# Latent attention of a two-layer decoder: the order of its query and key products, the split of the query weights, a shorter rotation and head loads in two parts

## The chip, the cores and the metric

The kernel runs on one core of a Trainium2 chip. The metric is device time in microseconds (us), the median of several runs. The profile shows one execution: PE is TensorE (matrix products), PEld its weight loads, DVE is VectorE, ACT is ScalarE, POOL is GpSimd, and SP is the engine that only issues transfers. ACT and POOL can issue transfers too. Each engine works through its own instructions in order; an instruction that waits holds up all that stand behind it on its engine.

## The reference

Two layers over 1024 positions of width 1024. The first layer mixes tokens by latent attention with 12 heads, the second by a sliding window; both have four heads of attention over a memory beside it and a squared-ReLU MLP behind. The change touches the first layer's mixer:

```python
def mla_mixer(hn, positions, w_in, q_norm_g, kv_norm_g, w_uq, w_ukv):
    proj = hn @ w_in
    c_q, c_kv, k_r, q_cross = ...
    q = (rmsnorm(c_q, q_norm_g) @ w_uq).reshape(b, s, 12, 96)
    q = concatenate([q[..., :64], rope(q[..., 64:], positions)])
    kv = (rmsnorm(c_kv, kv_norm_g) @ w_ukv).reshape(b, s, 12, 128)
    k_nope, v = kv[..., :64], kv[..., 64:]
    k = concatenate([k_nope, rope(k_r)])
    return causal_dense_attention(q, k, v), q_cross
```

`rope` rotates 32 values as two halves of 16: `x1 * cos - x2 * sin` and `x1 * sin + x2 * cos`. The softmax is over `q @ k.T / sqrt(96)` under a causal mask.

## The kernel before

Everything is float32. For products that need its precision, each operand is split into a high part (rounded to the format that PE takes at full rate) and a low part, the rest, and three products are summed: high by high, high by low, low by high. `split` (L96) makes the two parts: an ACT copy, scaled if there is a scale, writes the high part, and a DVE operation writes the low part. `part` (L931) does the same for a result in PSUM and sends the low part to DRAM through SP's queue, from a ring of four buffers named `lo`.

The stages of the first layer, with their times in the profile:

- `a_in` (34 to 131 us) projects each tile of 128 positions, normalises, rotates the 32 shared key values with `rope` (L317) and transposes. `rope` takes four DVE products of half width and two POOL additions.
- The values and the attention over the memory (131 to 176 us).
- The queries and keys (176 to 246 us), L945 to L1007, which is what the change rewrites. There are three kinds of product. The plain keys come from the compressed keys, pair of heads by pair of heads (`pskn`, j = 0 to 5, 12 products of 512 columns each, in one of two large PSUM buffers). The rotated part of the queries comes for each tile of positions t = 0 to 7 (`q_rope`, `psqr`, 9 products of 384 columns); `rope` rotates it on DVE and POOL, and two tiles later `q_ropeT` (`psqt`) transposes it on PE and parts it. The plain queries come for each pair of heads and half of the positions (`q_nope`, `psqn`, 12 times 9 products of 512 columns). The program writes them down as: all keys, then all rotated queries, then the plain queries. The order in which they stand on PE is made from this by a planner that fills a place where it expects an instruction not to be ready.
- The query weights are loaded by `load_cols` (L702) in 18 pieces, 9 of the rotated columns (`wqr`) and 9 of the plain ones (`wqn`), each through one of two buffers (`wr` in the profile, tag `wraw`). With `pool_too`, POOL scales the piece in place (L712), ACT rounds it (L713), POOL subtracts (L714), and only then is the buffer free for the next load, which SP issues (L707). `wqr` takes the place of the value weights; `wqn` takes the place of the key weights `wkn` as a whole, and one new tile.
- The attention proper (246 to 438 us) goes through 12 heads of 12 blocks each. A head's operands are four tiles (high and low of query and key, 96 rows and one row for a correction) in one of three sets of buffers. `head_tiles(h)` (L875) has SP issue up to eight loads into them: high and low, plain and rotated rows; the third set lies in space that the weights leave free only when the last query product is done. Before a head is attended to, its row maxima are found: `row_max(h, i)` (L900) multiplies high by high for the i-th tile of queries, and a DVE operation (L912) takes the maximum; when all eight are there, `max_row(h)` (L888) transposes them on PE (`psxt`), ACT copies them, and a transfer from ACT's queue puts them into the correction row. In the attention the order of PE's products is written out by hand: block n = 12h + j issues its scores (`pss`), then the row maxima that the table `WHEN` (L1195) puts there for a later head, then, every sixth block, a batch of products with the values (`pso`). Where a block crosses the diagonal, DVE adds the mask (L1076) for heads 2 to 8, PE for the others. POOL sums the probabilities (L1091).
- The sums of each head go through `den`; `rc_split` (L1168) inverts them for a group of heads on DVE, and `rc_mul` (L1176) multiplies the outputs, also on DVE, at places given by block number (L1234 to L1238).
- From 438 us on: the output projection, the MLP and the whole second layer, which the change leaves alone.

Of the kernel before, what the change touches and what calls it, by code (L numbers as in the profile page):

```python
# [19 lines left out]
P = 128  # L20
# [35 lines left out]
def trunk(  # L56
# [260 lines left out]
    def rope(pl, src, dst, t, nh, ab=None):  # L317

        rope_ct[0] += 1
        c = cosb[:, t : t + 1, :].to_broadcast([P, nh, 16])  # L320
        s = sinb[:, t : t + 1, :].to_broadcast([P, nh, 16])
        if ab is None:
            ab = [pl.tile([P, nh, 16], F32, tag=f"r{e}", bufs=2, name=f"r{e}{rope_ct[0]}") for e in "ab"]
        a, b = ab
        x1, x2 = src[:, :, 0:16], src[:, :, 16:32]
        V = nc.vector
        V.tensor_tensor(dst[:, :, 0:16], x1, c, ALU.mult)
        V.tensor_tensor(a, x2, s, ALU.mult)
        V.tensor_tensor(dst[:, :, 16:32], x1, s, ALU.mult)
        V.tensor_tensor(b, x2, c, ALU.mult)  # L330
        nc.gpsimd.tensor_tensor(dst[:, :, 0:16], dst[:, :, 0:16], a, ALU.subtract)
        nc.gpsimd.tensor_tensor(dst[:, :, 16:32], dst[:, :, 16:32], b, ALU.add)
# [369 lines left out]
    def load_cols(src, nk, w, outs, g, pool_too=False):  # L702

        for kt in range(nk):
            for i in range(3):
                raw = wu.tile([P, 4, w], F32, tag="wraw", bufs=2, name=f"wr{w}_{outs[0][1]}_{kt}_{i}")
                nc.sync.dma_start(out=raw.rearrange("p h c -> p (h c)"), in_=src[kt * P : (kt + 1) * P, i * 4 * w : (i + 1) * 4 * w])  # L707
                for dst, c0, n in outs:
                    o = [d[:, i * 4 * n : (i + 1) * 4 * n].rearrange("p (h c) -> p h c", c=n) for d in dst[kt]]
                    r = raw[:, :, c0 : c0 + n]  # L710
                    if pool_too:
                        nc.gpsimd.tensor_scalar(r, r, g[:, kt : kt + 1], None, ALU.mult)  # L712
                        nc.scalar.activation(o[0], r, AF.Copy)  # L713
                        nc.gpsimd.tensor_tensor(o[1], r, f32(o[0]), ALU.subtract)  # L714
                    else:
                        split(r, *o, scale=g[:, kt : kt + 1])
                yield
# [5 lines left out]
    loading = load_cols(mla_w_ukv[0], 2, 128, [(wkv, 64, 64), (wkn, 0, 64)], g_kv)  # L723

    CQC, CKR = 640, 896
    def a_in(t):
# [10 lines left out]
             [f1[:, t % 2, MLA_IN + 16 * i : MLA_IN + 16 * i + 16].rearrange("p (h c) -> p h c", h=1) for i in range(2)])  # L737
# [180 lines left out]
    kn = [kq[j // 4][:, j % 4, :] for j in range(6)]  # L918
    qr = [kq[1][:, 2, :], kq[1][:, 3, :], raw_tile([P, S], "qr2")]
# [58 lines left out]
    def q_ropeT(t):  # L978
# [197 lines left out]
    def rc_mul(c):  # L1176
# [30 lines left out]
    for n in range(len(seq) + 2):  # L1207
# [1146 lines left out]
```

## Time and profile before

| | |
|---|---|
| median of three runs | 2097.43 us (2095.31 to 2098.25) |
| profiled execution, own time | 2094.01 us |
| its span | 2092.2 us, so 1.8 us lie around it |
| mean granted clock | 0.997 |
| PE busy | 98% of the span |
| DVE, ACT, POOL busy | 68%, 51%, 13% |

The tables of stretches list, for a piece of the span, each engine's busy time and the number of its instructions, then the clock that PE was granted (1.00 is full speed), the busy share of the 16 DMA engines and the rate moved. The tables of waits list who waited for whom: total us, how many times, and the longest. In a timeline a row is start, duration, engine, line, operation, output and inputs with their shapes, the count, and in brackets the idle time before it with what ended it.

### The profile page before, as it was taken

How to read it: one execution, taken by the hardware profiler on the slowest of the kernel's cores; microseconds unless marked ns; L12 is line 12 of the kernel's file. 1: busy time of each engine (PE TensorE's matmuls, PEld its weight loads, DVE VectorE, ACT ScalarE, POOL GpSimd, SP SyncE). 2: the span in 40 equal slices, each digit the busy share in tenths (PEclk: the TensorE clock that was granted, in tenths of full speed). 3: DMA queues.
4: the chain of work that ended last, by engine and by line, in shares of the span. 5: the costliest groups of instructions: out<-in, count | busy, mean ns of one | idle time of the engine just before them, and what ended most of it. 6: DMA issues, size and time to landing. Idle time of an engine off the chain costs nothing.

```text
span 2092.2 us, 29674 instructions
## 1 busy us (share of the span) xinstructions
PE 2057.0 (98%) x10035; PEld 1677.8 (80%) x10035; DVE 1415.6 (68%) x2841; ACT 1072.0 (51%) x2349; POOL 276.9 (13%) x397
## 2 busy tenths in 40 slices
PE   8999899999999999999999999999999999999998
PEld 6987676678888888888888888778888888888887
DVE  8765555565977777976558534666977776976665
ACT  7554244465755544444445435766755444444453
POOL 1004355630000000000001133420000000000000
PEclk9999999999999999999999999999999999999999
DMA  6304645442344546944433534542345446944342
GB/s 224 104 7 125 197 101 138 122 162 81 136 149 158 166 146 230 331 136 154 141 116 106 151 98 126 140 132 86 124 155 165 162 141 231 330 144 156 117 123 88
DMA packets 192780, 308.61 MB, mean 148 GB/s; under 512 B 18863, under 2 KB 77684, under 8 KB 192628
## 3 DMA queue, kind: packets, MB, share of 16 engines
q1 hardware_dynamic: 184368, 287.97, 43.8%
q0 software_dynamic: 4144, 13.14, 1.7%
q10 hardware_dynamic: 4116, 5.61, 1.0%
q8 instruction: 79, 1.29, 0.3%
q14 instruction: 73, 0.60, 0.1%
HBM read 196.25 MB, written 89.57 MB: 137 GB/s over the span
## 4 chain that ended last, share of the span: by engine, by line
PE 92%; DVE 2%; ACT 2%; DMA 1%; POOL 1%; issue 1%; SPq 0%; ACTq 0%; DVEq 0%; POOLq 0%
PE psy L1926 6%; PE psy L1927 6%; PE psy L1928 6%; PE psu L1590 5%; PE psu L1589 5%; PE psu L1588 5%; PE psz L1926 4%; PE psz L1927 4%; PE psz L1928 4%; PE psv L1590 4%; PE psv L1589 4%; PE psv L1588 4%; PE pss L1044 3%; PE pswo L109 3%; PE pswo L111 3%; PE pswo L110 3%
## 5 line engine op out<-in xcount | busy, mean ns | idle before, releaser
L99 ACT ACTIVATE g<-i 128x512 fp32r<-128x512 f32 x79 | 49.9, 631 | 103.7 <-PE psy L1927 52.2
L1926 PE MATMUL psy<-g 128*128 128x512 f32 x256 | 100.0, 390 | 0.0
L1927 PE MATMUL psy<-g 128*128 128x512 f32 x256 | 99.7, 389 | 0.0
L1928 PE MATMUL psy<-g 128*128 128x512 f32 x256 | 99.7, 389 | 0.0
L1078 ACT ACTIVATE p<-pss 128x512 f32<-128x512 f32 (+2 forms) x144 | 64.2, 491 | 68.2 <-PE pss L1044 31.9
L912 DVE CUSTOM_DVE_ANT_0 psx<-psx,wide 128x1024 f32<-128x1024 f32 (+7 forms) x96 | 72.9, 765 | 37.6 <-PE psx L910 36.7
L1091 POOL TENSOR_TENSOR acc<-p,acc 128x512 f32<-128x512 f32 (+2 forms) x96 | 89.4, 938 | 33.4 <-ACT p L1078 29.5
L100 DVE TENSOR_TENSOR g<-i,g 128x512 fp32r<-128x512 f32 x79 | 55.5, 703 | 49.5 <-ACT g L99 49.5
L99 ACT ACTIVATE uh<-i 128x512 fp32r<-128x512 f32 x66 | 41.7, 632 | 88.1 <-PE psz L1927 39.4
L99 ACT ACTIVATE i<-mr 128x512 fp32r<-128x512 f32 x78 | 47.8, 628 | 71.9 <-PE psy L1927 23.0
L100 DVE TENSOR_TENSOR uh<-i,uh 128x512 fp32r<-128x512 f32 x66 | 45.5, 690 | 48.8 <-ACT uh L99 48.8
L1926 PE MATMUL psz<-g 128*128 128x512 f32 x192 | 74.7, 389 | 0.0
L1927 PE MATMUL psz<-g 128*128 128x512 f32 x192 | 74.7, 389 | 0.0
L1928 PE MATMUL psz<-g 128*128 128x512 f32 x192 | 74.7, 389 | 0.0
L1487 ACT ACTIVATE mr<-mr,gcol 128x256 f32<-128x256 f32 (+1 forms) x160 | 63.8, 476 | 12.7 <-DMA mr<-in_mlp_w_up_dram 12.7
L2046 POOL TENSOR_TENSOR wsr<-wsr,gcol 128x1024 f32<-128x1024 f32 x12 | 23.4, 1947 | 342.5 <-ACT i L99 274.9
L100 DVE TENSOR_TENSOR i<-mr,i 128x512 fp32r<-128x512 f32 x78 | 53.5, 686 | 20.9 <-ACT i L99 20.8
L1808 DVE TENSOR_TENSOR mqq<-mqf,mqq 128x512 f32<-128x512 f32 x64 | 43.1, 686 | 22.4 <-DMA mqf<-in_mlp_w_down_dram 22.3
L1044 PE MATMUL pso<-p,v 128*64 128x256 f32 (+1 forms) x480 | 56.4, 380 | 0.0
L1928 PEld LDWEIGHTS psy<-g 128*128 128x128 f32 x256 | 48.0, 188 | 10.0
L1926 PEld LDWEIGHTS psy<-g 128*128 128x128 f32 x256 | 48.1, 188 | 9.9
L1927 PEld LDWEIGHTS psy<-g 128*128 128x128 f32 x256 | 48.1, 188 | 9.8
(661 smaller groups left out, 6775.3 us busy)
## 6 DMA issues: line engine op xcount, KB each, us to landing
i<-hd SPq DMA_DIRECT2D x154, 256.0 KB
hd<-uh SPq DMA_DIRECT2D x76, 256.0 KB
hd<-ul SPq DMA_DIRECT2D x76, 256.0 KB
mr<-in_mlp_w_up_dram SPq DMA_DIRECT2D x36, 512.0 KB
hd<-x SPq DMA_DIRECT2D x72, 256.0 KB
mr<-hd SPq DMA_DIRECT2D x70, 256.0 KB
d<-in_mlp_w_up_dram SPq DMA_DIRECT2D x32, 512.0 KB
mqf<-in_mlp_w_down_dram SPq DMA_DIRECT2D x32, 512.0 KB
```

Of the source, the lines that this page charges most:

```text
L99: a = nc.scalar.activation(hi, src, AF.Copy)
L100: d = nc.vector.tensor_tensor(lo, src, f32(hi), ALU.subtract)
L912: nc.vector.tensor_tensor_reduce(ps[:, :n], ps[:, :n], wide[h > 1][:, S - n :], -1.0, 3.0e38, ALU.add, ALU.min, accum_out=m)
L1044: last_mm[0:1] = [nc.tensor.matmul(*args, skip_group_check=True, **kw).ins]
L1078: masked[0:1] = [nc.scalar.activation(p[:, c0:], ps, AF.Exp, scale=SC).ins]
L1091: nc.gpsimd.tensor_tensor(a[:, c0:], p[:, c0:], (a if q is None else q)[:, c0:], ALU.add)
L1588: nc.tensor.matmul(ps, wh[:, k, :], xh[:, k, :], start=p in (1, 2, 5) and k == 0, stop=False, skip_group_check=True)
L1589: nc.tensor.matmul(ps, wh[:, k, :], xl[:, k, :], start=False, stop=False, skip_group_check=True)
L1590: nc.tensor.matmul(ps, wl[:, k, :], xh[:, k, :], start=False, stop=k == 3, skip_group_check=True)
L1926: nc.tensor.matmul(ps, ah[:, j, :], bh, start=start, stop=False, skip_group_check=True)
L1927: nc.tensor.matmul(ps, ah[:, j, :], bl, start=False, stop=False, skip_group_check=True)
L1928: nc.tensor.matmul(ps, al[:, j, :], bh, start=False, stop=k == NP - 1, skip_group_check=True)
```

## The change

The rotation works on both halves at once: two DVE products of full width (by cosine and by sine) instead of four of half width; POOL's two additions stay.

The query weights are split as all others are: ACT scales and rounds, DVE scales and subtracts. POOL computes nothing there any more and issues the loads instead of SP. All nine rotated pieces are written down before the first key product. The plain pieces 0 and 1 of each group take the place of the key weights column by column, as soon as the products that read those columns are done, and come in the order in which the queries need them.

The products alternate in the program: keys 0 to 2, then for each tile a rotated product with, after t = 0, 1, 2, keys 3 to 5, and after t = 4, 5, 6 a plain query. The rotated queries' three transposed blocks lie side by side and are parted in one go (384 columns) rather than two (256 and 128).

A head's loads come in two parts, first the high tiles, one step later the low ones, with the constant rows for the correction behind the low ones. The first row maxima of head 0 come three plain queries later. In `WHEN`, row maxima 3 to 0 come one block earlier, the transpose of the maxima one block later, and head 2's first two row maxima one block later. The normalisation of the first two groups of heads starts 4 and 3 blocks later, of the third one block later.

```diff
-        c = cosb[:, t : t + 1, :].to_broadcast([P, nh, 16])
-        s = sinb[:, t : t + 1, :].to_broadcast([P, nh, 16])
+        c = cosb[:, t : t + 1, :].to_broadcast([P, 2 * nh, 16])
+        s = sinb[:, t : t + 1, :].to_broadcast([P, 2 * nh, 16])
...
-        V.tensor_tensor(dst[:, :, 0:16], x1, c, ALU.mult)
-        V.tensor_tensor(a, x2, s, ALU.mult)
-        V.tensor_tensor(dst[:, :, 16:32], x1, s, ALU.mult)
-        V.tensor_tensor(b, x2, c, ALU.mult)
-        nc.gpsimd.tensor_tensor(dst[:, :, 0:16], dst[:, :, 0:16], a, ALU.subtract)
-        nc.gpsimd.tensor_tensor(dst[:, :, 16:32], dst[:, :, 16:32], b, ALU.add)
+        nc.vector.tensor_tensor(flat(dst), flat(src), c, ALU.mult)
+        nc.vector.tensor_tensor(flat(ab), flat(src), s, ALU.mult)
+        nc.gpsimd.tensor_tensor(dst[:, :, 0:16], dst[:, :, 0:16], ab[:, :, 16:32], ALU.subtract)
+        nc.gpsimd.tensor_tensor(dst[:, :, 16:32], dst[:, :, 16:32], ab[:, :, 0:16], ALU.add)
...
-    def load_cols(src, nk, w, outs, g, pool_too=False):
...
+    def load_cols(src, todo, w, outs, g, dma):
+
+        for kt, i in todo:
+            raw = wu.tile([P, 4, w], F32, tag="wraw", bufs=2, name=f"wr{w}_{outs[0][1]}_{kt}_{i}")
+            dma.dma_start(out=raw.rearrange("p h c -> p (h c)"), in_=src[kt * P : (kt + 1) * P, i * 4 * w : (i + 1) * 4 * w])
+            for dst, c0, n in outs:
+                o = [d[:, i * 4 * n : (i + 1) * 4 * n].rearrange("p (h c) -> p h c", c=n) for d in dst[kt]]
+                split(raw[:, :, c0 : c0 + n], *o, scale=g[:, kt : kt + 1])
+            yield
...
-    def head_tiles(h):
+    def head_tiles(h, lo):
...
-        if h in (1, 2):
-            head_ones(h)
-        for t, n, rope in ((kh, kn[h // 2][r, :], krh_d), (qh, qn[h // 2][r, :], qr[h // 4][e, :]), (kl, kn_d[r_, :], krl_d), (ql, qn_d[r_, :], qr_d[e_, :])):
+        for t, n, rope in ((kl, kn_d[r_, :], krl_d), (ql, qn_d[r_, :], qr_d[e_, :])) if lo else ((kh, kn[h // 2][r, :], krh_d), (qh, qn[h // 2][r, :], qr[h // 4][e, :])):
             nc.sync.dma_start(out=f32(t[0:64]), in_=n)
...
+        if h in (1, 2) and lo:
+            head_ones(h)
...
-    kn = [kq[j // 4][:, j % 4, :] for j in range(6)]
-    qr = [kq[1][:, 2, :], kq[1][:, 3, :], raw_tile([P, S], "qr2")]
+    kn = [kq[j // 4][:, j % 4, :] for j in range(5)] + [raw_tile([P, S], "kn5")]
+    qr = [kq[1][:, 1 + j, :] for j in range(3)]
...
-    for j in range(6):
-        if j == 1:
-            wqr = rows(wpair(wu, 3, 384, "wqr", "b"), 3)
-            for _ in load_cols(mla_w_uq[0], 3, 96, [(wqr, 64, 32)], g_q, True):
-                pass
+    wqr = rows(wpair(wu, 3, 384, "wqr", "b"), 3)
+    for _ in load_cols(mla_w_uq[0], [(kt, i) for kt in range(3) for i in range(3)], 96, [(wqr, 64, 32)], g_q, nc.gpsimd):
+        pass
+    wqn = wkn + rows(wpair(wu2, 1, 768, "wqn2", "c"), 1)
+    loading = load_cols(mla_w_uq[0], [(kt, i) for i in range(3) for kt in range(3)], 96, [(wqn, 0, 64)], g_q, nc.gpsimd)
+
+    def k_nope(j):
...
-        part(kq[1][:, 2:4, sl], pt[:, 0 : 2 * P].rearrange("p (k c) -> p k c", k=2), qr_d[0 : 2 * P, sl].rearrange("(k p) c -> p k c", p=P))
-        part(qr[2][:, sl], pt[:, 2 * P : 3 * P], qr_d[2 * P : 3 * P, sl])
-
+        part(kq[1][:, 1:4, sl], pt.rearrange("p (k c) -> p k c", k=3), qr_d[:, sl].rearrange("(k p) c -> p k c", p=P))
+
+    for j in range(3):
+        k_nope(j)
     for t in range(NT):
         q_rope(t)
-        for _ in range(1 + (t < 2)):
-            next(loading, None)
+        if t < 3:
+            k_nope(t + 3)
+        if t < 5:
+            for _ in range(2 if t < 4 else 1):
+                next(loading, None)
         if t > 1:
             q_ropeT(t - 2)
-    q_nope(0, 0)
+        if t in (4, 5, 6):
+            q_nope((t - 4) // 2, t % 2)
     q_ropeT(NT - 2)
-    q_nope(0, 1)
+    q_nope(1, 1)
     q_ropeT(NT - 1)
-    head_tiles(0)
-    for n in range(2, 12):
+    for n in range(4, 12):
         q_nope(n // 2, n % 2)
-        for i in range(2 * n - 4, min(2 * n - 2, NT)):
-            row_max(0, i)
         if n == 4:
-            head_tiles(1)
-        if n == 8:
+            head_tiles(0, 0)
+        if n == 5:
+            head_tiles(0, 1)
+        if n == 7:
+            head_tiles(1, 0)
+        if n == 9:
+            head_tiles(1, 1)
+        if 4 < n < 9:
+            for i in range(2 * n - 10, 2 * n - 8):
+                row_max(0, i)
+        if n == 9:
             max_row(0)
...
-        1: ((4, 0), (3, 1), (2, 2), (1, 3), (0, 4), (8, 6)),
-        2: ((7, -5), (6, -4), (5, -1), (4, 1), (3, 2), (2, 3), (1, 4), (0, 5), (8, 6)),
+        1: ((4, 0), (3, 1), (2, 2), (1, 3), (0, 4), (8, 7)),
+        2: ((7, -4), (6, -3), (5, -1), (4, 1), (3, 1), (2, 2), (1, 3), (0, 4), (8, 7)),
+        3: ((7, -5), (6, -4), (5, -1), (4, 1), (3, 1), (2, 2), (1, 3), (0, 4), (8, 7)),
...
-            if j == 0 and h + 2 < H:
-                head_tiles(h + 2)
+            if j < 2 and h + 2 < H:
+                head_tiles(h + 2, j)
...
-        for c in range(3):
-            if n == GRP[c + 1] * NB + (8 if c == 2 else 10):
+        for c, (a, b) in enumerate(((6 * NB + 14, 6 * NB + 17), (11 * NB + 1, 11 * NB + 4), (11 * NB + 9, 11 * NB + 10))):
+            if n == a:
                 rc_split(c)
-            if n == GRP[c + 1] * NB + (9 if c == 2 else 13):
+            if n == b:
                 muls = rc_mul(c)
```

More of the change, by code (lines that the diff above doesn't have):

```diff
@@ L319, in rope, with flat @@
         rope_ct[0] += 1
-        c = cosb[:, t : t + 1, :].to_broadcast([P, nh, 16])
-        s = sinb[:, t : t + 1, :].to_broadcast([P, nh, 16])
+        c = cosb[:, t : t + 1, :].to_broadcast([P, 2 * nh, 16])
+        s = sinb[:, t : t + 1, :].to_broadcast([P, 2 * nh, 16])
         if ab is None:
[L323 to L328, printed above, removed]
-        V.tensor_tensor(dst[:, :, 16:32], x1, s, ALU.mult)
-        V.tensor_tensor(b, x2, c, ALU.mult)
-        nc.gpsimd.tensor_tensor(dst[:, :, 0:16], dst[:, :, 0:16], a, ALU.subtract)
-        nc.gpsimd.tensor_tensor(dst[:, :, 16:32], dst[:, :, 16:32], b, ALU.add)
+            ab = pl.tile([P, nh, 32], F32, tag="ra", bufs=2, name=f"ra{rope_ct[0]}")
+        def flat(ap):
+            return ap.rearrange("p h (e c) -> p (h e) c", e=2)
+        nc.vector.tensor_tensor(flat(dst), flat(src), c, ALU.mult)
+        nc.vector.tensor_tensor(flat(ab), flat(src), s, ALU.mult)
+        nc.gpsimd.tensor_tensor(dst[:, :, 0:16], dst[:, :, 0:16], ab[:, :, 16:32], ALU.subtract)
+        nc.gpsimd.tensor_tensor(dst[:, :, 16:32], dst[:, :, 16:32], ab[:, :, 0:16], ALU.add)
     class MemKV:
@@ L700, in wpair @@
         return [pl.tile([P, k, n], F32R, tag=f"{slot}{e}", name=f"{name}{e}") for e in "hl"]
-    def load_cols(src, nk, w, outs, g, pool_too=False):
[L704 to L717, printed above, removed]
+    def load_cols(src, todo, w, outs, g, dma):
[6 more added lines that the diff above has]
+            yield
     def rows(w, n):
@@ L722, in trunk @@
     wkn, wkv = rows(wpair(wu, 2, 768, "wkn", "a"), 2), rows(wpair(wu, 2, 768, "wkv", "b"), 2)
-    loading = load_cols(mla_w_ukv[0], 2, 128, [(wkv, 64, 64), (wkn, 0, 64)], g_kv)
+    loading = load_cols(mla_w_ukv[0], [(kt, i) for kt in range(2) for i in range(3)], 128, [(wkv, 64, 64), (wkn, 0, 64)], g_kv, nc.sync)
     CQC, CKR = 640, 896
@@ L736, in a_in @@
         rope(pa, ps[:, 640:672].rearrange("p (h c) -> p h c", h=1), c[:, CKR : CKR + 32].rearrange("p (h c) -> p h c", h=1), t, 1,
-             [f1[:, t % 2, MLA_IN + 16 * i : MLA_IN + 16 * i + 16].rearrange("p (h c) -> p h c", h=1) for i in range(2)])
+             f1[:, t % 2, MLA_IN : MLA_IN + 32].rearrange("p (h c) -> p h c", h=1))
         cs_[t] = c
@@ L949, in trunk @@
         nc.sync.dma_start(out=krh_d[:, c], in_=hi)
-    for j in range(6):
-        if j == 1:
-            wqr = rows(wpair(wu, 3, 384, "wqr", "b"), 3)
-            for _ in load_cols(mla_w_uq[0], 3, 96, [(wqr, 64, 32)], g_q, True):
-                pass
+    wu2 = pool("wu2", "right")
+    wqr = rows(wpair(wu, 3, 384, "wqr", "b"), 3)
[4 more added lines that the diff above has]
+    def k_nope(j):
         ps = ps2(f"pskn{j}")
@@ L959, in trunk @@
             part(kn[j][:, s], ps[:, s], kn_d[j * P : (j + 1) * P, s])
-    wu2 = pool("wu2", "right")
-    wqn = rows(wpair(wu, 2, 768, "wqn", "a"), 2) + rows(wpair(wu2, 1, 768, "wqn2", "c"), 1)
-    loading = load_cols(mla_w_uq[0], 3, 96, [(wqn, 0, 64)], g_q, True)
     def q_nope(j, i):
@@ L1200, in trunk @@
     for h in range(1, H):
-        for i, d in WHEN[min(h, 2)]:
+        for i, d in WHEN[min(h, 3)]:
             ahead.setdefault((h - 1) * NB + d, []).append((h, i))
```

## The prediction, made before the changed kernel was run

> **What bounds the kernel now.** I read the table of stretches first, cut at the stages. The columns are busy us of PE, PEld, DVE, ACT and POOL with instruction counts, then PE's granted clock.
>
> ```profile
> 176.00:198.00 22.00, 20.09 (x92) 16.34 (x90) 9.21 (x17) 8.87 (x20) 9.63 (x17) 1.00 0.72 229
> 198.00:213.00 15.00, 11.29 (x65) 9.37 (x64) 9.24 (x33) 4.12 (x14) 14.60 (x22) 1.00 0.45 123
> 213.00:246.00 33.00, 30.92 (x136) 23.37 (x133) 18.89 (x44) 10.05 (x23) 7.35 (x13) 1.00 0.66 186
> 246.00:262.00 16.00, 12.02 (x58) 8.69 (x60) 5.96 (x15) 4.59 (x10) 6.14 (x6) 0.83 0.72 215
> 262.00:438.00 176.00, 166.45 (x1129) 122.35 (x1125) 95.16 (x237) 81.95 (x188) 110.66 (x114) 0.99 0.48 117
> 438.00:2092.00 1654.00, 1646.79 (x7623) 1352.95 (x7621) 1148.99 (x2118) 854.71 (x1802) 112.98 (x156) 1.00 0.48 153
> ```
>
> PE is the bound everywhere, and from 438 us on it is idle 7.2 us in 1654. So whatever the front saves or loses goes through to the end one for one; the change can move nothing behind 438. Ahead of that PE is idle, stretch by stretch, 1.9 + 3.7 + 2.1 + 4.0 + 9.6 = 21.3 us. That, and two stretches at a lower clock, is all the change can win by removing waits. In 198 to 213 another engine is the bound: POOL is busy 14.6 of 15 us. Next, PE's rows of the table of waits, for 160 to 262 us and for 262 to 438 us.
>
> ```profile
> PE psx L910 <- DMA qh<-kq: 3.6, 1, 3.6
> PE psqt L983 <- POOL fa L332: 2.4, 4, 0.8
> PE pskn L118 <- DVE lo L942: 1.9, 3, 0.9
> PE pss L1044 <- DVE lo L942: 1.7, 1, 1.7
> PE psqt L983 <- POOL wqnl L714: 0.9, 1, 0.9
> PE psqt L983 <- POOL wqn2l L714: 0.7, 1, 0.7
> PE psqt L983 <- DVE lo L942: 0.4, 1, 0.4
> ```
>
> ```profile
> PE psxt L891 <- DVE m L912: 6.1, 8, 2.3
> PE psx L910 <- DVE m L912: 1.5, 3, 0.9
> PE psxt L891 <- ACT p L1078: 1.1, 2, 0.5
> ```
>
> These name three places. A, the queries and keys: 1.9 us of key products behind evictions, and 2.4 + 0.9 + 0.7 + 0.4 = 4.4 us of transposes (`psqt`) behind POOL. B, head 2's first row maximum: one wait of 3.6 us for its load. C, the attention: 6.1 + 1.1 = 7.2 us of `psxt`, ten waits, one a head. The clock adds to B and C; the timeline of PE and the stretches behind those two waits show it.
>
> ```profile
> 257.82 4.96 PE L1044 MATMUL pso<-p,v 128*64 128x256 f32 x24
> ...
> 335.17 2.60 PE L1044 MATMUL pso<-p,v 128*64 128x256 f32 x24
> ...
> 384.01 3.62 PE L1044 MATMUL pso<-p,v 128*64 128x256 f32 x24
> ```
>
> ```profile
> 256.70:262.70 6.00, 6.00 (x26) 3.14 (x26) 1.29 (x2) 0.00 (x0) 0.00 (x0) 0.50 0.56 150
> 382.00:388.00 6.00, 6.00 (x41) 3.37 (x39) 2.42 (x4) 1.07 (x4) 3.99 (x4) 0.72 0.46 106
> ```
>
> The same batch of 24 value products takes 2.60 us as a rule, 4.96 us behind the wait of 3.6 us and 3.62 us behind the `psxt` wait of 2.3 us; the granted clock there is 0.50 and 0.72. The 6.0 us at 0.50 lose 3.0 us, the 6.0 us at 0.72 lose 1.7 us; I price them 2.9 and 1.5, since a rest of the stretch is not PE's bound.
>
> **The change part by part.** The rotation. The rows are those of the groups by line, 173 to 246 us.
>
> ```profile
> L327 DVE TENSOR_TENSOR fa<-psqr,trig 128x192 f32<-128x192 f32 x8 | 2.8, 350 | 0.5 <-PE psqr L111 0.4
> ...
> L942 DVE TENSOR_TENSOR lo<-psqt,qr 128x128 f32<-128x128 f32 x8 | 2.3, 290 | 9.2 <-ACT qr L941 9.2
> ```
>
> Four products of 192 columns and 350 ns become two of 384. From 128 to 192 columns these rows rise by 60 ns, so 384 should take about 350 + 180 = 530 ns: 1.40 - 1.06 = 0.34 us a tile, 2.7 us of DVE in all. DVE is busy 9.2 of 22 and 9.2 of 15 us there, so on the path this is worth nothing by itself. With the parting in one go (one `lo`, one store less a tile) it frees what the weights now take of DVE: 9 splits of 128 columns at 290 ns and 9 of 256 at about 410 by the same slope, 6.3 us over some 30 us. Cost zero, covered by DVE's idle half; if the cover were gone, it would be 6.3 - 2.7 = 3.6 us.
>
> The weights. From the same view, POOL's first addition of the rotation:
>
> ```profile
> L331 POOL TENSOR_TENSOR fa<-fa,ra 128x192 f32<-128x192 f32 x8 | 4.8, 600 | 1.0 <-DVE ra L328 1.0
> ```
>
> POOL loses all its scalings and subtractions and keeps two such additions of 0.6 us a tile plus the load issues. So the 4.4 us of `psqt` should go: between a rotated product and its transpose now lie two tiles with a key or plain query product each, 3 us or more of PE work a tile, and the chain between is 1.1 us on DVE and 1.2 us on POOL. Of the 1.9 us of `pskn`, the first three keys still follow each other, so 0.5 us stays and 1.4 us goes. A saves 5.8 us before its new wait.
>
> The new wait is the place to work out. All nine rotated pieces must be there for the first rotated product, and they now go through POOL's queue. Four views: the groups on the tile `wr`, the page's list of transfers, the times to landing of the tile `xd`, and POOL's timeline at the start.
>
> ```profile
> L713 ACT ACTIVATE wqrh<-wr x9: 301/311/313, 173.4 to 191.8; 128x128 fp32r<-128x128 f32 x9
> L714 POOL TENSOR_TENSOR wqrl<-wr,wqrh x9: 454/459/464, 173.8 to 192.1; 128x128 fp32r<-128x128 f32 x9
> ```
>
> ```profile
> xd<-i POOLq DMA_DIRECT2D x32, 256.0 KB, 2.3
> ```
>
> ```profile
> DMA to landing us min/median/max: 2.3/2.3/5.3
> ```
>
> ```profile
> 4.55 0.57 POOL L145 DMA_DIRECT2D sinks_b<-in_swa_sinks_dram  x1
> ...
> 12.44 0.26 POOL L146 TENSOR_SCALAR sinks_b<-sinks_b 128x12 f32<-128x12 f32 x1 [5.09 <-DMA sinks_b<-in_swa_sinks_dram]
> ```
>
> Today the nine run from 173.4 (when the value weights' place comes free) to 192.6 us. A load of this size from POOL's queue is not in the trace; the nearest row is the store of 256 KB, 2.3 us from issue to landing, at most 5.3, and the far end is the load at the start, 7.9 us (4.55 to 12.44, in the rush of first loads). I take 2.3. A buffer's round is then 2.3 + 0.31 (ACT) + 0.29 (DVE) + 0.3, 3.2 us; the 0.3 are three hand-overs of the 0.1 us that lie between the first ACT row (173.4 + 0.31) and POOL's first (173.8). The DVE split with a scale is not in the trace at this width: 0.29 is the plain subtraction, POOL's 0.46 the other end, 0.7 us more in four rounds. Two pieces wait in the buffers, so the ninth comes four rounds after 174.0: 186.8 us. The nine plain pieces follow at the same pace, a pair in 3.2 us and some more for their width, so near 203 us, ahead of most of their products. When does PE need the ninth? These rows of PE's timeline give its pace and its freedom.
>
> ```profile
> 178.94 0.39 PE L119 MATMUL pskn<-ckl,wknh 128*128 128x512 f32 x1
> 179.17 0.61 PE L121 MATMUL pskn<-ckh,wknl 128*128 128x512 f32 x2
> 179.62 0.33 PE L109 MATMUL psqr<-wqrh,cTh 128*128 128x384 f32 x1
> ```
>
> A key product starts every 0.23 us (178.94, 179.17). At 179.62 keys 0 and 1 are through; key 2 takes 12 x 0.23 = 2.8 us and the 0.5 us of wait that stay: 182.9. If the rotated product stands right behind, PE waits 3.9 us and pays the slow clock, 6.8 us together. But the rotated product at 179.62, in the middle of the keys, shows that the order on PE isn't the program's: where the planner expects a product to wait, it puts a later one. Then keys 3 to 5 fill in, 8.3 us, to 191.2, and the wait is nothing. I take that, with 0.8 us for small new gaps: **A saves 5 us**. Its bounds: 1.0 us lost (3.9 + 2.9 - 5.8) and 8 us saved, the whole idle time of the stage.
>
> B. SP's timeline has two of head 2's constant rows, ahead of its first load; the chain of waits has the last load that the product needs.
>
> ```profile
> 248.32 0.54 SPq L872 DMA_DIRECT2D kh<-kh  x1
> 248.92 0.57 SPq L872 DMA_DIRECT2D kl<-kl  x1
> ```
>
> ```profile
> 252.70 3.76 DMA qh<-kq
> ```
>
> These two rows now go behind the low tiles, so the four loads ahead of the product can leave 1.2 us earlier (248.32 to 249.49), and the last lands at 255.3 instead of 256.5. The product itself stands one block later, three or four score products of 0.23 us, 0.7 us at least. The wait of 3.6 us shrinks by 1.9 to 1.7 us; that is shorter than the 2.3 us that still cost clock, so the 2.9 us go as well: 4.8, say **B saves 5 us**. Between 0 (SP held up by something else, such as the last stores of `lo`) and 6.5. The wait of 1.7 us for `lo` at the stage's end stays.
>
> C. Row maxima 3 to 0 leave one block earlier and `psxt` one later, two blocks of 0.7 us or more against ten waits that but for one are some 0.5 us: they go. The one of 2.3 us had DVE's multiplications of the outputs (`rc_mul`) ahead of it; they move to other blocks, and `psxt` has room. Of 7.2 us I take 6.2, add the clock's 1.5 and take off 1.2 for what is late next, DVE's maxima ahead of `psx` (1.5 us today) with the multiplications in new places. **C saves 6.5 us**, between 2 and 9. Its cover is the time from `psxt` to the next head's first scores: the transfer of the maxima still has about four blocks and a batch of values to land in.
>
> A rule of the Trainium skill bears on the clock: "TensorE: Matmul & The Clock Gate", Part 1, lets PE's clock fall to half after an idle window of about 3.4 us. The wait of 3.6 us agrees; that of 2.3 us fell short of it and the clock still went to 0.72, so the trace decides. By the page alone, C would be 1.5 us less and the sum 15 us.
>
> Sum: 5 + 5 + 6.5 = 16.5 us. Against the profiled execution, 2094.0 us, that gives 2077.5. The median of the three runs is 3.4 us above that execution; the forecast is for the median, 2097.4 - 16.5 = **2081 us**, by itself 2074 to 2087.
>
> **The rivals.**
> 1. POOL's loads land late. At 5.3 us, the longest of the stores, a round is 6.2 us and the ninth piece comes at 198.8: PE, with all keys done, waits 7.6 us from 191.2 and pays 2.9 us of clock. A loses 10.5 - 5.8 = 4.7 us, B and C win 11.5: 2091 us. For it: nothing in the trace shows these loads at 2.3. Against it: only the maximum of 32 stores is that long. The Trainium skill has a cause, "SBUF — State Buffer", the box on DVE blocking DMA: GpSimd cannot write its descriptors while DVE runs a copy or the like in a two-port mode, and an example grows from 0.62 to 3.1 us. The DVE rows of this stage are subtractions, products and maxima out of PSUM, no such copy between SBUF tiles, so the trace gives it little room.
> 2. Slower. The same loads, but PE's order keeps the rotated product right behind three keys. At the 7.9 us of the start a round is 8.8 us and the ninth piece comes at 209.2: PE waits 26.3 us from 182.9, plus 2.9, less 5.8 and 11.5: 11.9 us slower, 2109. It decides from a landing of 6 us (wait 18.6 us, 4 us slower). For it: the first rotated product is now written ahead of keys 3 to 5. Against it: the row at 179.62.
> 3. The loads of head 2 gain nothing, because SP's queue is held by the stores behind DVE, or C's waits come back behind DVE: one of B and C is lost, 2086 to 2088.
> 4. The alternation does nothing (PE's order was already mixed), POOL's waits turn into DVE's, and B's wait stays above 2.3 us and keeps its clock: within 4 us of before, 2094 to 2099.
>
> **How the numbers follow.** A measurement of this kernel can tell about 0.2%, 4.2 us, from no change. Chances: the forecast 0.57, rival 1 0.12 (two thirds of it clearly faster), rival 2 0.09, rival 3 0.13, rival 4 0.09. Faster: 0.57 + 0.08 + 0.13 = 0.78; the same: 0.04 + 0.09 = 0.13; slower 0.09. The range runs from 2070 (A 8, B 6.5 and C 9 would be 2074, and the three runs spread by 3) to 2096, which leaves out rival 2 and half of rival 4.
>
> **What would show it.** A: no `psqt` wait for POOL, the last split of the rotated weights near 187 us, rotated products among the keys, the first `pss` near 241 us instead of 246.4. Wrong if PE stands before the first `psqr`. B: the wait of `psx` for `qh` under 2 us and a granted clock of 1.00 behind it. C: no `psxt` in the table of waits, a batch of values at 2.6 us in every head. Behind the output projection's first product every stage should last as long as before; if one does not, the accounting is wrong.

## The result, and the profile after

| | changed kernel | kernel before |
|---|---|---|
| median (4 runs each, same chip) | 2081.66 us (2079.11 to 2083.47) | 2096.37 us (2093.91 to 2098.25) |
| profiled execution, and its span | 2081.73 us, 2079.8 us | 2094.01 us, 2092.2 us |

The ratio is 0.993 with a 95% interval of 0.9912 to 0.9947: 14.7 us faster, between 11 and 18. The forecast was 2081 us. The time agrees; the places don't. The forecast gave 5 us to A (the queries and keys), 5 us to B (head 2's loads), 6.5 us to C (the attention). Four starts on PE cut both traces at the same work: the last products of the memory's scores (`psco`), the first score product (`pss`), the first batch of 24 value products (`pso`) for head 1, and the first product of the output projection (`pswo`). PE's timeline of the kernel before:

```profile
173.05 1.95 PE L474 MATMUL psco<-cpT,vm0b 128*64 128x256 f32 x16
...
246.41 0.50 PE L1044 MATMUL pss<-qh,kh 97*128 97x512 f32 x1 [1.66 <-DVE lo L942]
...
275.46 2.60 PE L1044 MATMUL pso<-p,v 128*64 128x256 f32 x24
...
438.24 0.50 PE L109 MATMUL pswo<-woq,x 128*128 128x512 f32 x1
```

And of the changed kernel:

```profile
173.43 1.95 PE L473 MATMUL psco<-cpT,vm0b 128*64 128x256 f32 x16
...
247.65 0.40 PE L1047 MATMUL pss<-qh,kh 97*128 97x512 f32 x1
...
270.93 2.60 PE L1047 MATMUL pso<-p,v 128*64 128x256 f32 x24
...
425.06 0.50 PE L109 MATMUL pswo<-woq,x 128*128 128x512 f32 x1
```

Subtracting one start from the next gives the time of each stretch:

| stretch | before | after | saved | forecast |
|---|---|---|---|---|
| start to `psco` | 173.05 | 173.43 | -0.4 | 0 |
| `psco` to the first `pss` (A) | 73.36 | 74.22 | -0.9 | 5 |
| the first `pss` to head 1's values (B) | 29.05 | 23.28 | 5.8 | 5 |
| head 1's values to `pswo` (C) | 162.78 | 154.13 | 8.7 | 6.5 |
| `pswo` to the end | 1653.96 | 1654.74 | -0.8 | 0 |

The sum is 12.4 us, the difference of the two spans. The table of stretches of the changed kernel, cut as in the prediction (busy us of PE, PEld, DVE, ACT, POOL with counts, then PE's granted clock), shows why A gained nothing:

```profile
176.00:198.00 22.00, 18.44 (x72) 14.80 (x71) 9.54 (x20) 7.31 (x16) 4.47 (x8) 0.84 0.65 193
198.00:213.00 15.00, 10.93 (x55) 9.67 (x54) 9.97 (x21) 6.25 (x13) 7.92 (x15) 0.91 0.71 211
213.00:246.00 33.00, 33.00 (x159) 27.55 (x159) 21.37 (x43) 10.10 (x19) 5.09 (x9) 0.99 0.61 182
246.00:262.00 16.00, 14.82 (x90) 11.87 (x89) 8.16 (x20) 6.63 (x15) 8.23 (x11) 1.00 0.62 167
262.00:438.00 176.00, 173.09 (x1159) 128.31 (x1158) 105.50 (x258) 86.41 (x200) 109.80 (x113) 1.00 0.53 136
```

From 213 to 246 us PE is full, and from there to the projection the clock is 1.00. Ahead of 213 us PE is idle 3.6 and 4.1 us, and the clock is 0.84 and 0.91. The largest waits of PE, for 160 to 250 us and for 250 to 440 us:

```profile
PE psqt L975 <- DVE lo L934: 4.1, 1, 4.1
PE psqr L109 <- ACT wqrh L102: 3.3, 1, 3.3
...
```

```profile
PE psx L902 <- DVE m L904: 2.5, 5, 0.9
...
```

All ten `psxt` waits, head 2's wait for `qh`, the waits of `psqt` for POOL and the 1.7 us of `pss` for `lo` are gone. The waits of `psx` for DVE's maxima have grown from 1.5 to 2.5 us. In A two large waits have come, and PE is slow behind both (stretches):

```profile
187.20:193.40 6.20, 6.15 (x16) 4.94 (x17) 2.44 (x5) 1.77 (x4) 1.61 (x3) 0.52 0.68 196
...
210.80:213.80 3.00, 3.00 (x9) 2.51 (x10) 2.68 (x6) 1.19 (x3) 2.52 (x5) 0.53 0.75 206
```

About half of these 9.2 us, 4.4 us by the clocks, is lost on top of the 7.4 us of waiting. Where the first wait comes from is read in two timelines, POOL's issues and ACT's splits:

```profile
178.63 0.54 POOL L705 DMA_DIRECT2D wr<-in_mla_w_uq_dram  x1 [2.72 <-DVE wqrl L103]
179.71 0.54 POOL L705 DMA_DIRECT2D wr<-in_mla_w_uq_dram  x1 [0.55 <-DVE wqrl L103]
182.69 0.54 POOL L705 DMA_DIRECT2D wr<-in_mla_w_uq_dram  x1 [2.44 <-DVE wqrl L103]
```

```profile
181.60 0.40 ACT L102 ACTIVATE wqrh<-wr,gcol 128x128 fp32r<-128x128 f32 x1 [0.81 <-DMA wr<-in_mla_w_uq_dram]
...
186.80 0.40 ACT L102 ACTIVATE wqrh<-wr,gcol 128x128 fp32r<-128x128 f32 x1 [4.31 <-DMA wr<-in_mla_w_uq_dram]
...
188.81 0.40 ACT L102 ACTIVATE wqrh<-wr,gcol 128x128 fp32r<-128x128 f32 x1 [1.12 <-DMA wr<-in_mla_w_uq_dram]
...
194.09 0.39 ACT L102 ACTIVATE wqrh<-wr,gcol 128x128 fp32r<-128x128 f32 x1
```

The first issue shown was split by ACT 3.0 us later, the second 7.1 us, the third 6.1 us. The view of the tile `wr` has the times from issue to landing of the loads through POOL:

```profile
DMA to landing us min/median/max: 2.6/3.1/7.1
```

These are the fifth, sixth and seventh of the nine rotated pieces. The first wait is for the sixth, split at 186.80: the first rotated product had been begun with the pieces before it. The ninth was split at 194.1 us; the forecast had it done at 186.8. The second wait starts in DVE's timeline (`wkn` holds plain query weights by now, in the place of the key weights):

```profile
205.30 0.49 DVE L103 SCALAR_TENSOR_TENSOR wknl<-wr,gcol,wknh 128x256 fp32r<-128x256 f32 x1 [2.51 <-ACT wknh L102]
...
207.74 0.48 DVE L103 SCALAR_TENSOR_TENSOR wknl<-wr,gcol,wknh 128x256 fp32r<-128x256 f32 x1
209.66 0.48 DVE L103 SCALAR_TENSOR_TENSOR wqn2l<-wr,gcol,wqn2h 128x256 fp32r<-128x256 f32 x1 [1.44 <-ACT wqn2h L102]
210.06 0.55 DVE L934 TENSOR_TENSOR lo<-psqt,kq 128x384 f32<-128x384 f32 x1
```

The `lo` at 210.06 parts the first transposed tile, which PE finished at 203.2. It stands in DVE's line behind splits of plain weights whose pieces aren't there yet, and the third tile's `psqt` (210.76) waits for its buffer. PE itself doesn't need those plain weights yet: a late piece stops it through DVE's line.

### The profile page after: what moved, and what is told of

It reads as the page before. It is cut to its first block, busy times and chain, and to the rows that moved or that the text cites. A ratio compares the mean times of both kernels' runs of the same rounds, so it can differ in the third digit from the quotient of the medians.

```text
span 2079.8 us, 29586 instructions
## 1 busy us (share of the span) xinstructions
PE 2053.5 (99%) x10035; PEld 1678.8 (81%) x10035; DVE 1419.9 (68%) x2819; ACT 1071.5 (52%) x2341; POOL 264.1 (13%) x379
## 4 chain that ended last, share of the span: by engine, by line
PE 94%; DVE 2%; issue 1%; DMA 1%; ACT 1%; POOL 0%; ACTq 0%; DVEq 0%; POOLq 0%
PE psu L1594 6%; PE psu L1593 6%; PE psu L1592 6%; PE psy L1932 6%; PE psy L1930 6%; PE psy L1931 6%; PE psz L1931 4%; PE psz L1930 4%; PE psz L1932 4%; PE psv L1594 4%; PE psv L1593 4%; PE psv L1592 4%; PE pss L1047 4%; PE pswo L111 3%; PE pswo L109 3%; PE pswo L110 3%
## 5 line engine op out<-in xcount | busy, mean ns | idle before, releaser
L1081 ACT ACTIVATE p<-pss 128x512 f32<-128x512 f32 (+2 forms) x144 | 64.2, 491 | 50.7 <-DVE pss L1079 20.7
L1491 ACT ACTIVATE d<-d,gcol 128x256 f32<-128x256 f32 x128 | 53.6, 498 | 0.0
```

The source lines that it names most:

```text
L1491: nc.scalar.activation(w[:, k, :], w[:, k, :], AF.Copy, scale=g_mlp[layer][:, k0 + k : k0 + k + 1])
```

## The experiments

Theory 1: A gained nothing because its loads come late through POOL's queue, and B and C made all of the 14.7 us. Theory 2: A saved its 5 us as forecast, and B and C less than it seems. Each ratio is against the kernel before on the same chip; "saved" is one minus the ratio, times the 2095.5 to 2095.8 us of the kernel before.

**One half at a time: `bc_only` and `a_only`.** `bc_only` is the kernel before with the whole attention part of the change, of which these are the main lines; the other rows of `WHEN` and the lines of `rc_split` and `rc_mul` are as in the change too:

```diff
-    def head_tiles(h):
+    def head_tiles(h, lo):
...
-        1: ((4, 0), (3, 1), (2, 2), (1, 3), (0, 4), (8, 6)),
+        1: ((4, 0), (3, 1), (2, 2), (1, 3), (0, 4), (8, 7)),
...
-            if j == 0 and h + 2 < H:
-                head_tiles(h + 2)
+            if j < 2 and h + 2 < H:
+                head_tiles(h + 2, j)
```

> The kernel before with only the attention part of the change: a head's loads in two parts, constant rows behind them, row maxima one block earlier, psxt one block later, the output multiplications in other blocks. The queries and keys stage is as before. Theory 1 (the stage of queries and keys gained nothing from the change: the changed kernel's two new waits, 3.3 and 4.1 us, with slow clock behind both, eat the waits it lost): 13 to 16 us under before, so equal to the changed kernel or up to 3 us below it. Theory 2 (the stage did save its 5 us, as forecast): 8 to 11 us under before, 4 us or more above the changed kernel. By both: psx waits for qh under 1 us, no psxt in the waits of the attention.

`a_only` is the changed kernel with `WHEN`, `rc_split` and `rc_mul` as before, and head 2's loads in one go again:

```diff
-            if j < 2 and h + 2 < H:
-                head_tiles(h + 2, j)
+            if j == 0 and h + 2 < H:
+                if h == 0:
+                    head_ones(2)
+                head_tiles(h + 2, 0)
+                head_tiles(h + 2, 1)
```

> The changed kernel with the attention's timing and head 2's loads as before, so that only the stage of queries and keys differs from before. Theory 1: the same as before within 3 us, with the two waits of 3.3 and 4.1 us (psqr for ACT's wqrh, psqt for DVE's lo) still there and the psxt waits of 7 us back. Theory 2: 5 us under before.

Measured: `bc_only` 2080.45 us, ratio 0.9938 (0.9924 to 0.9952), 13.0 us saved; `a_only` 2095.34 us, ratio 1.000 (0.9991 to 1.0009), nothing saved within 1.9 us. Theory 2 falls: A by itself is worth nothing, where the forecast said 5 us. `bc_only`'s profiled execution, at 2085.71 us its longest, shows something else. Its timeline at the first score product, and its stretches behind it:

```profile
246.71 0.50 PE L1046 MATMUL pss<-qh,kh 97*128 97x512 f32 x1 [1.66 <-DVE lo L942]
```

```profile
246.00:256.00 10.00, 9.29 (x29) 8.18 (x30) 4.97 (x15) 3.18 (x7) 3.24 (x3) 0.59 0.92 258
256.00:264.00 8.00, 7.87 (x42) 5.22 (x40) 0.57 (x1) 1.87 (x6) 3.50 (x5) 0.66 0.14 32
```

The wait for `qh` is gone, but the clock falls all the same, now behind the 1.66 us at the stage's end. By the times, not in each execution: three executions took 2079.2 to 2080.5 us at a mean clock of 0.999 to 1.000, two took 2085.2 and 2085.7 us at 0.996.

**The attention's two parts: `b_only` and `c_only`.** Both start from the kernel before.

```diff
-        2: ((7, -5), (6, -4), (5, -1), (4, 1), (3, 2), (2, 3), (1, 4), (0, 5), (8, 6)),
+        2: ((7, -4), (6, -3), (5, -1), (4, 1), (3, 2), (2, 3), (1, 4), (0, 5), (8, 6)),
+        3: ((7, -5), (6, -4), (5, -1), (4, 1), (3, 2), (2, 3), (1, 4), (0, 5), (8, 6)),
```

That, with the split `head_tiles`, is `b_only`.

> The kernel before with a head's loads in two parts, the constant rows of head 2 behind them, and head 2's first two row maxima one block later; everything else as before. As forecast: 5 us under before, a psx wait for qh of 1.7 us left and no slow clock behind it. By the trace of the changed kernel (wait and clock both gone): 6 to 7 us. If only the earlier maxima and the later psxt of the other part made the 15 us: within 2 us of before.

`c_only` has the other edits of `WHEN` and those of `rc_split` and `rc_mul`:

```diff
-        2: ((7, -5), (6, -4), (5, -1), (4, 1), (3, 2), (2, 3), (1, 4), (0, 5), (8, 6)),
+        2: ((7, -5), (6, -4), (5, -1), (4, 1), (3, 1), (2, 2), (1, 3), (0, 4), (8, 7)),
```

> The kernel before with the row maxima one block earlier, psxt one block later and the output multiplications in other blocks; head 2's loads and its first two maxima as before, with its wait of 3.6 us. As forecast: 6.5 us under before. By the distance of head 1's second batch of values to the last head's in the two traces (140.05 us before, 131.69 us in the changed kernel): 8.4 us. If it hangs on the other part: under 4 us.

Measured: `c_only` 2084.38 us, ratio 0.9944 (0.993 to 0.9958), 11.7 us saved (8.8 to 14.7): above the forecast's 6.5. Its trace tells where. All ten traces with C's edits (some of these runs stand further down) take 153.8 to 154.8 us from head 1's values to `pswo` (154.2 in `c_only`). Without them the profile of the kernel before takes 162.78 us, but `a_only`, `b_only` and `a_sp` take 164.2 to 164.8: behind the longest `psxt` wait, 2.3 to 2.4 us, the clock of 382 to 394 us was 0.86 in the kernel before, which loses 1.7 us, and 0.72 in `a_only` and `b_only`, which loses 3.4. So C is worth 8.7 to 10.7 us by the traces. The wait of `psx` for `qh`, which `c_only` was to keep, isn't there: by its stretches PE was slow ahead of that place, which gave the load time.

```profile
246.00:256.00 10.00, 8.63 (x29) 7.59 (x30) 5.64 (x15) 3.24 (x7) 3.27 (x3) 0.66 0.65 211
256.00:264.00 8.00, 8.00 (x39) 5.17 (x38) 1.29 (x2) 1.34 (x4) 2.95 (x3) 0.57 0.62 166
```

`b_only` 2095.81 us, ratio 0.9996 (0.9986 to 1.0005): nothing. Yet its wait is gone; its timeline and its stretches tell what came for it:

```profile
260.43 0.68 PE L910 MATMUL psx<-kh,qh 96*128 96x512 f32 x2 [0.90 <-DVE m L912]
...
263.10 2.34 PE L1046 MATMUL pss<-ckh,ckl 97*128 97x512 f32 x5
```

```profile
256.00:264.00 8.00, 6.95 (x44) 5.37 (x41) 3.11 (x5) 1.97 (x6) 5.40 (x6) 0.90 0.46 107
264.00:272.00 8.00, 8.00 (x38) 5.80 (x37) 2.27 (x7) 2.17 (x5) 0.54 (x2) 0.67 0.82 209
```

The largest wait in the 12 us ahead is 0.90 us, and PE is slow from 262 to 269 us. Of eleven executions three kept a mean clock of 0.998 or more and took 2088.8 to 2091.1 us, 4 to 7 us under before; the others, at 0.997 or less, took 2093.5 to 2098.8. The traces agree: of the ten with B's edits, seven take 23.2 to 23.9 us from the first `pss` to head 1's values, with a whole clock, and `bc_only`, `b_only` and `sp_three` 26.5 to 29.3, with a slow one (27.8 to 29.1 without B's edits). So B's saving is there only where the clock holds.

**The wait at the stage's end: `seam1`.** One line of `bc_only`:

```diff
-        if n == 8:
+        if n == 9:
             max_row(0)
```

> The run bc_only (before with only the attention part of the change) with one line moved: head 0's psxt one query product later (n == 9, as in the changed kernel, for n == 8), by which the first score product no longer takes the buffer that DVE's lo frees last. In bc_only PE waits 1.66 us there (246.71) and then runs at a clock of 0.59 and 0.66 until 262, as it did behind head 2's load before. If that wait starts the slow clock: wait and slow clock gone, 1.7 + 6 us under bc_only, 2071 to 2075. If the clock falls there for another reason (a sum of many small gaps ahead, the switch to attention): only the wait goes, 2078 to 2081, and a slow stretch near 250 to 270 stays.

Measured: 2080.67 us (2078.50 to 2081.34), ratio 0.9925 (0.9912 to 0.9937). The trace has a wait of 0.4 us there, and the clock stays whole:

```profile
246.00:256.00 10.00, 9.47 (x58) 7.33 (x58) 5.57 (x15) 5.18 (x11) 5.21 (x8) 1.00 0.81 236
256.00:264.00 8.00, 6.93 (x45) 5.41 (x41) 3.92 (x7) 2.84 (x7) 4.78 (x6) 1.00 0.59 134
```

From the first `pss` (246.46) to head 1's values (270.39) are 23.93 us, as in the changed kernel, for 29.30 in the profile of `bc_only`. The medians are equal, since three of five executions of `bc_only` kept their clock; what `seam1` lacks are the two at 0.996 (its five lie at 0.997 to 1.000). Five executions a side, on two chips, don't show that the wait starts the slow clock. The run does show where the changed kernel lost its wait of 1.7 us, which the forecast let stand: by the place of one `psxt`.

**Who carries the loads: `sp_loads` and `act_loads`.**

```diff
-    for _ in load_cols(mla_w_uq[0], [(kt, i) for kt in range(3) for i in range(3)], 96, [(wqr, 64, 32)], g_q, nc.gpsimd):
+    for _ in load_cols(mla_w_uq[0], [(kt, i) for kt in range(3) for i in range(3)], 96, [(wqr, 64, 32)], g_q, nc.sync):
```

The same in the second `load_cols`, and `nc.scalar` in `act_loads`.

> The changed kernel with the eighteen query weight loads issued by SP and not by POOL; nothing else. If it is POOL's queue that makes them late (landing 3.1 us median and 7.1 at most, DMA descriptors written by software), the waits of 3.3 and 4.1 us shrink to under 1 us each and the clock stays at 1.00: 7 to 10 us under the changed kernel. If it is the two buffers and the in-order splits on ACT and DVE, whatever queue issues: within 3 us of the changed kernel, with a psqr or psqt wait of 3 us or more left. If SP's in-order queue holds the loads behind stores that wait for DVE: slower than the changed kernel by 3 us or more.

> The changed kernel with the eighteen query weight loads issued by ACT. It tells whether a load lands late because POOL's queue is slow, or because it isn't in one line with SP's stores of lo and shares the DMA engines with them (five of 256 KB leave between 179 and 187 us, and the loads issued at 179.71 and 182.69 took 7.1 and 6.1 us to ACT's split). If POOL's queue is slow: longest load 4.8 us as on SP, and the time near the 2074 of SP's loads. If it is the sharing: again 6 us or more for the loads issued among the stores, and 2078 or more. ACT's own waits for the buffers, ahead of its evictions, can add to both.

Measured: `sp_loads` 2074.21 us, ratio 0.9901 (0.9887 to 0.9914), 20.7 us saved; `act_loads` 2076.01 us, ratio 0.9906 (0.9893 to 0.992), 19.7 us saved. So issuing through POOL is what made them late. The waits of `sp_loads` in 160 to 250 us:

```profile
PE psqr L109 <- ACT wqrh L102: 1.8, 1, 1.8
PE psqn L109 <- DVE ra L329: 1.8, 1, 1.8
```

They shrink from 7.4 to 3.6 us, not to under 1 us each as expected, and the clock holds at 1.00. The edit also takes the issues out of POOL's own line, where one stood about 1 us behind the rotation's additions (at 198.55 in the changed kernel); the late loads of the first wait stood behind none. `act_loads` separates the queue from the traffic: SP's stores run beside it, as they do beside POOL. The five transfers of 256 KB are these in SP's timeline of the changed kernel (in `act_loads` they leave between 177.88 and 182.29 us); then ACT's line in `act_loads`:

```profile
179.19 0.34 SPq L935 DMA_DIRECT2D knd<-lo  x1
179.81 0.55 SPq L872 DMA_DIRECT2D kh<-kq  x1
180.80 2.76 SPq L935 DMA_DIRECT2D knd<-lo  x3
```

```profile
181.23 1.41 ACTq L705 DMA_DIRECT2D wr<-in_mla_w_uq_dram  x2
...
185.81 0.40 ACT L102 ACTIVATE wqrh<-wr,gcol 128x128 fp32r<-128x128 f32 x1 [2.52 <-DMA wr<-in_mla_w_uq_dram]
```

The first of the two loads issued from 181.23, among the stores, is split 4.6 us later, where POOL's took 7.1 and 6.1; the longest rotated one on SP took 4.8.

**More buffers: `three_raw` and `sp_three`.**

```diff
-            raw = wu.tile([P, 4, w], F32, tag="wraw", bufs=2, name=f"wr{w}_{outs[0][1]}_{kt}_{i}")
+            ct[0] += 1
+            pl, tag, nb = (wu2, "wraw2", 1) if w == 96 and ct[0] % 3 >= 2 else (wu, "wraw", 2)
+            raw = pl.tile([P, 4, w], F32, tag=tag, bufs=nb, name=f"wr{w}_{outs[0][1]}_{kt}_{i}")
```

`sp_three` has this and SP's loads.

> The changed kernel with three buffers for a raw piece of the query weights instead of two (the third from the right-hand pool beside them). If the round of two buffers paces the loads: a piece every 1.5 us instead of 2.2, the second row block of the rotated weights there about 3 us earlier, the psqr wait of 3.3 us gone and the psqt wait of 4.1 us halved, 5 to 9 us under the changed kernel. If the transfers themselves are the pace (shared with the stores of lo): within 2 us.

> The changed kernel with SP's loads and three buffers together. If both take away the same two waits (1.8 us each are left with SP's loads, 1.9, 1.3 and 0.5 us with three buffers): 2070 to 2073, with at most 1 us of waits between 176 and 246 us. If three buffers put more loads in one go ahead of the stores in SP's line, and the stores hold the lo buffers: no better than 2074.

Measured: `three_raw` 2076.76 us, ratio 0.9912 (0.9899 to 0.9926), 18.4 us saved; `sp_three` 2070.28 us, ratio 0.9883 (0.987 to 0.9897), 24.5 us saved. A third buffer hides most of POOL's lateness (waits of 1.9, 1.3 and 0.5 us left, a clock of 0.72 from 186 to 192 us behind the first). Both together are the best version here, 0.5% under the changed kernel by the ratios; its stretch A is 64.02 us (`psco` 173.36, `pss` 237.38) for 74.22. It still waits more than expected, 1.8 us in A for the 1 us expected; the second row below is a row maximum in B, behind which the clock fell in this execution, the slowest of the four:

```profile
PE psqt L979 <- DVE lo L938: 1.6, 1, 1.6
PE psx L906 <- DVE m L908: 0.9, 1, 0.9
...
```

**A by itself, with loads in time: `a_sp`.** It is `a_only` with `nc.sync` in both loads.

> The run a_only (before with only the queries and keys part of the change) with the eighteen loads issued by SP. The forecast's working for this part (4.4 us of psqt and 1.4 us of pskn waits go, loads that land in 2.3 to 3 us, 5 us saved) is tested by itself. If it holds for loads that land in time: 2088 to 2091, 5 to 8 us under a_only, with the wait for qh of 3.5 us, its slow clock and the psxt waits still there. If it doesn't, and the gain of SP's loads hangs on the attention part: within 2 us of a_only.

Measured: 2087.31 us, ratio 0.996 (0.9948 to 0.9973), 8.4 us saved (5.7 to 10.9). The waits from 160 to 250 us:

```profile
PE psx L902 <- DMA qh<-kq: 3.6, 1, 3.6
PE psqn L109 <- DVE ra L329: 1.4, 1, 1.4
PE psqr L109 <- ACT wqrh L102: 0.5, 1, 0.5
```

Head 2's wait of 3.6 us is B's, and still there, as are the `psxt` waits (7.2 us). Stretch A takes 64.34 us (173.07 to 237.41), 9.0 us less than before.

**The order on PE: `keys_first`.**

```diff
-    for j in range(3):
+    for j in range(6):
         k_nope(j)
...
-        if t < 3:
-            k_nope(t + 3)
```

> The changed kernel with all six keys written ahead of the first rotated product, so that PE's line holds all the key products (but for two or three rotated ones) in front: the order that the forecast assumed. If the order on PE was the error (keys 3 to 5 stood behind a rotated product that waited): the psqr wait of 3.3 us and its slow clock go, 5 us or more under the changed kernel. If the late landing was it (the ninth piece split at 194.1 us, the keys done near 191): a wait of 3 us at another place, within 3 us of the changed kernel.

Measured: 2079.93 us, ratio 0.9923 (0.991 to 0.9937), 16.1 us saved for the changed kernel's 14.7: no difference that can be told. The wait of `psqr` is gone and another has come:

```profile
PE pskn L118 <- DVE lo L934: 3.1, 3, 2.3
PE psqt L975 <- DVE lo L934: 1.8, 1, 1.8
PE psqt L975 <- POOL fa L331: 1.4, 1, 1.4
PE psqn L109 <- DVE ra L329: 0.4, 1, 0.4
```

The longest wait of the keys, 2.3 us, is for an eviction on DVE, which stands behind a split whose piece is late. The order the forecast assumed would have changed little.

**The rotation: `oldrope`.** The changed kernel with the four products of before:

```diff
-        nc.vector.tensor_tensor(flat(dst), flat(src), c, ALU.mult)
-        nc.vector.tensor_tensor(flat(ab), flat(src), s, ALU.mult)
+        V.tensor_tensor(dst[:, :, 0:16], x1, c, ALU.mult)
+        V.tensor_tensor(a, x2, s, ALU.mult)
+        V.tensor_tensor(dst[:, :, 16:32], x1, s, ALU.mult)
+        V.tensor_tensor(b, x2, c, ALU.mult)
```

> The changed kernel with the rotation as four products of 192 columns again (4 x 350 ns for 2 x 550 ns a tile, measured). Forecast: worth nothing on the path, within 2 us of the changed kernel. Rival: DVE, which takes its splits, partings and rotations in one line, is late in this stage, so that 0.3 us a tile come out on PE: 2.4 us slower, or more where a wait grows past what holds the clock.

Measured: 2081.18 us, ratio 0.9933 (0.9921 to 0.9946): the changed kernel's time. The shorter rotation is worth nothing that can be measured, as forecast.

## Why the prediction was right, and where it was wrong

**The sum** came out by luck: errors cancel. A was forecast 5 us too high (5 for nothing in `a_only`), C 2 us too low by the two traces and up to 5 by `c_only`. In the two traces they cancel only in part, 12.4 us for 16.5; the profile of the kernel before was one of its faster executions, so the medians lie 14.7 us apart. And the median of three that the sum was taken from, 2097.4, came down to 2096.4 with the fourth run.

**A, wrong.** The step that failed is "I take 2.3" for a load through POOL's queue, and the round of 3.2 us built on it. The median was 3.1 us, and the sixth and seventh rotated pieces, issued among SP's stores, took 7.1 and 6.1; the ninth moved from 186.8 to 194.1 us. That the first rotated product must have all nine was wrong too: it was begun with the first three, and stopped for the sixth. Three further steps rested on loads in time:
- "Then keys 3 to 5 fill in ... and the wait is nothing": they did not. PE's line held the rotated products behind keys 0 to 2, and a case like the one priced beside it came (3.9 us and 2.9 of clock; measured 3.3 and 3.0). That the sizes agree is chance: the forecast's wait was for the ninth piece, this one for the sixth. `keys_first` shows that the other order would have waited as well.
- The plain pieces "ahead of most of their products", hence free: it was their splits that made the larger wait, 4.1 us.
- "Cost zero, covered by DVE's idle half": DVE had the time, but it works in one line, and a split whose piece is late holds up partings that PE needs.

What A removes was rather sized too low: with loads on SP it saves 8.4 us by the runs, 9.0 by the stretch, of which the forecast counted 5 and let the 1.7 us at the stage's end stand.

**B, right in size in the two traces, wrong in its reason.** There it is 5.8 us for 5. But the step "shorter than the 2.3 us that still cost clock, so the 2.9 us go as well" failed: the clock fell behind 1.66 us in `bc_only` and behind 0.90 us in `b_only`. B alone was worth nothing in most executions. The wait it should have left, 1.7 us, was zero; that the wait of 0.9 us for DVE's maxima, which came in its place, cost no clock in the changed kernel was luck.

**C, right in mechanism, too small.** All ten `psxt` waits went. Of the 1.2 us taken off for DVE's maxima, 1.0 came in the changed kernel (`psx` waits 2.5 us for 1.5), but not by C: `c_only` has 1.2 us, and 0.9 of the 2.5 lie in B. The clock's 1.5 us fit the profile of the kernel before (1.7 lost there), but `a_only` and `b_only` lost 3.4 us in that place. And a wait costs more than its idle time here: the batches of values at 290.45 and 305.24 before are 14.79 us apart with a `psxt` wait of 0.54 us between; the same two in the changed kernel (285.25, 299.37) are 14.12 apart without it. That is 0.67 for 0.54, and the next pair has 0.72 for 0.54; why isn't shown.

**The rivals.** The first two share what came: the loads were late as in the first (5.3 us, 2091), in the order on PE of the second (a rotated product behind three keys). What kept the time at 2081 is, by the stretches, that only two loads of nine took over 6 us, and that C gave more. The third and the fourth did not come. Of the signs, these held: no `psqt` wait for POOL, no `psxt`, a clock of 1.00 and 2.60 us a batch in the attention. PE did stand before a `psqr`, and the first `pss` came at 247.65 for 241: these two told A's failure. The stages behind `pswo` kept their length within 0.8 us.

## What to carry to other kernels

- Ask of a load in a ring of two buffers not only when PE needs the data, but what stands behind its consumer on that consumer's engine. A late piece stopped PE twice here, once through weights it needed and once through an eviction that stood behind weights it didn't need.
- Move a load to another queue only with that queue's times under the traffic of that moment. Here the one word `nc.sync` for `nc.gpsimd`, at the same work, was worth 6 to 8 us of the 2080.
- Judge a removed wait by several executions and their clocks: one profile can show a slow stretch that most executions don't have.

## What the runs showed of the hardware that was not expected

- **POOL's queue among other transfers.** With five transfers of 256 KB leaving SP between 179 and 184 us (178 and 182 in `act_loads`), loads of 192 KB took 7.1 and 6.1 us through POOL and 4.6 through ACT; with the loads in SP's own line, among the same stores, 4.8. An issue of these loads occupies POOL for 0.54 us, SP and ACT for 0.34 (medians). The Trainium skill, "Perfetto Trace Analysis", section "DMA Instruction — SWDGE (GPSIMD)", says that the end shown for such an issue is the end of writing descriptors, not of the transfer; the trace agrees (0.54 us, and landing at 2.6 us at the least). Why the queue falls behind among stores stays open. Two rows speak against DVE in the way, the cause weighed with the first rival, though DVE's new splits do read SBUF tiles: the issue of the load of 7.1 us took 0.54 us like the others (all eighteen 0.54 to 0.63), and in the last 2.9 us of that load, from 183.90 us on, DVE did nothing:

```profile
183.90:187.20 3.30, 0.03 (x1) 0.00 (x0) 0.00 (x0) 0.40 (x2) 0.00 (x0) 0.87 0.81 285
```

- **The clock falls behind short waits, and not always.** In the profile of `bc_only` it fell behind 1.66 us and stayed low for some 14 us (248 to 261), longer than behind the 3.57 us of the kernel before (6 us); `c_only` shows the same (249 to 263). It held behind the same 1.66 us in the profile of the kernel before. Behind 0.90 us it fell in `b_only`, and behind 0.91 us, at 259.69 us, it held at 1.00 in the changed kernel. Behind a wait of 1.8 us in A it held in `sp_loads` and fell in `act_loads` (0.73 from 204 to 210 us). "TensorE: Matmul & The Clock Gate" of the Trainium skill, Part 1, asks for an idle window of about 3.4 us; the 3.3 and 4.1 us here fit that, the falls behind 1.66 and 0.90 us don't. What decides between them isn't settled by these runs.
